# Last chunk of the second down projection: four token tiles in pairs, four one by one, the last one in column halves

## The chip, the cores and the metric

One core of a Trainium2 chip runs the whole program. The metric is the device time of one execution in microseconds. Engines are named as the profile names them: PE (TensorE matmuls), PEld (TensorE weight loads), DVE (VectorE), ACT (ScalarE), POOL (GpSimd) and SP (SyncE, whose queue issues nearly all DMAs).

## The reference, cut to what matters

The reference is one inference step of a two-layer decoder trunk on 1024 prompt tokens and 64 sample tokens, width 1024, in float32. Each layer ends in a convolutional feed-forward block:

```
def conv_ffn(x, buf, w_up, conv_w, conv_b, w_down):
    h = x @ w_up                                  # 1024 -> 2 x 2816
    ...                                           # 3-tap causal convolution over tokens -> hc
    gate, val = jnp.split(hc, 2, axis=-1)
    out = (jax.nn.gelu(gate) * val) @ w_down      # 2816 -> 1024
    return out, hp[:, -(CONV_W - 1):]
...
x = x + rmsnorm(f_out, p['f_post_g'][i])
```

The change touches the product with w_down of the second layer, its root-mean-square norm with the gain f_post_g, and the residual addition, which give the outputs y_prompt and y_sample and are the last work of the program.

## The kernel before, in words

**Numbers in two parts.** Every float32 operand of a large matmul is split into a high part (fp32r) and the rest (lo). ACT casts the high part (L150), DVE subtracts it (L151). A product is three matmuls: high by high, high by low, low by high (mm3, L815, L816, L817).

**The down projection** (class Down, function ffn_down). The 2816 rows of w_down are 22 blocks of 128, in six chunks: blocks 0 and 1, then five chunks of four. Tokens are eight tiles of 128 (numbers 0 to 7) and the tile NTT of 64 sample tokens. Each chunk adds its part of the sum to a float32 tile acc per token tile. A chunk of kind "p" is computed plainly, tile by tile (function plain): per tile 4 blocks x 3 matmuls x 2 column halves = 24 matmuls, and 2 additions of a PSUM tile to acc. A chunk of kind "s" uses a Strassen-type scheme on pairs of token tiles (function pair): blocks two by two, columns in halves, tokens in two tiles, and seven products in place of eight. A pair takes 7 products x 2 block pairs x 3 = 42 matmuls of 128x512, and 7 additions to acc (function add, L1437), with PSUM tiles that go on accumulating after an addition has read them. Before the change the second layer's last chunk is of kind "s", in the order LORD = (NTT, 0, 2, 4, 6), where 0 stands for the tiles 0 and 1, and so on. The first layer's last chunk is of kind "p".

**Staging.** The input of a step comes from a DRAM buffer gd through the SP queue. For a pair and each of two block pairs, stage loads a tile gr of 256 KB (L1363), POOL makes four sums and differences of it (L1368 to L1371), and ACT and DVE split seven 128x128 operands in three pieces of 256, 128 and 512 columns. For a plain step, stage loads 256 KB (L1350; L1354 for the sample tile) and splits 512 columns at once. The weights of a "s" chunk are b11, b21, b22 and four differences t1 to t4, per block pair, each 128x512; b12 itself is not kept.

**The tail of a token tile** (function tail_a, L847 to L861, from done). ACT squares acc and sums it (L830), DVE multiplies by the gain (L857), forms the mean (L121), ACT takes the root (L126), DVE the reciprocal and one refining step (L127, L136, L140), DVE scales and adds the residual (L860), and SP stores the tile (L861). A residual tile is fetched four tiles ahead (fetch, L1392). For tile 7 the gain, the scaling and the store go by halves of the columns.

**What sets the order.** The functions emit instructions in program order; a list scheduler then fixes the order on each engine: instructions that are ready and have their buffers come first by program order, so an instruction can be hoisted far ahead of its place in the program. Each engine and the SP queue then runs its list strictly in that order. Buffers: gr has 5 slots (loads, sums of POOL, the junk output of the squares), acc has 14 (accumulators, gain, some staged operands), xr and raw 2 each, PSUM 5 for products. In ffn_down, pairs emit the staging of the next step and the tails of earlier tiles after two of their seven products; after the last pair (tt == 6) the tails of the tiles 4 to 7 come behind all matmuls in program order.

Of the kernel before, what the change touches and what calls it, by code (L numbers as in the profile page):

```python
# [20 lines left out]
P = 128  # L21
# [52 lines left out]
def trunk_kernel(ctx, tc, I, O):  # L74
# [772 lines left out]
    def tail_a(y, tt, post, xsrc, xdst, last=False, rest=slice(0, D), aside=False, xr=None):  # L847


        t0, n = tokens(tt)  # L850
        if xr is None:
            xr = slot("xr")
            nc.sync.dma_start(xr[0:n], xsrc(tt))
        halves = (slice(512, D), slice(0, 512)) if last else (slice(0, D),)
        ss = square_sum(y[:, rest], n)
        for hs in halves if last else (rest,):
            V.tensor_tensor(y[:, hs], y[:, hs], post[0:n, hs], ALU.mult)  # L857
        r = rstd_from(pools["ph"], ss, 1, n, "n1", bufs=4, pre=sums.pop(tt, None), aside=aside, root=tail.root)
        for hs in halves:
            V.scalar_tensor_tensor(y[:, hs], y[:, hs], r[0:n], xr[0:n, hs], op0=ALU.mult, op1=ALU.add)  # L860
            nc.sync.dma_start(xdst(tt)[:, hs], y[:, hs])  # L861
# [213 lines left out]

    NPAR = 20
    NCV = 18
    LORD = (NTT, 0, 2, 4, 6)

    def conv_params(i):  # L1080

# [173 lines left out]
    class Down:  # L1255
# [6 lines left out]
        def __init__(self, i):  # L1262
            self.wv = I["w_down"][i].rearrange("(f p) d -> p f d", p=P)
            last = i == 0
            self.plan = [("p", 0, 2)] + [("s", f, 4) for f in (2, 6, 10, 14)] + [("p" if last else "s", 18, 4)]
            self.steps = []
            for c, (kind, f0, nf) in enumerate(self.plan):
                self.steps += [(c, tt) for tt in (ORDER if kind == "p" else LORD if c == len(self.plan) - 1 else (0, 2, 4, NTT, 6))]
            self.gx, self.ws, self.loads = {}, {}, {}
            fh, fl = [t.rearrange("p k t -> p (k t)") for t in (xh, xl)]  # L1270
            self.xq = [fh[:, 1024 * j : 1024 * j + 1024] for j in range(7)]
            self.xp = [fl[:, 1024 * j : 1024 * j + 1024] for j in range(3)]
            cut = lambda t, o, n: t[:, o : o + n]
            self.pc = [cut(fl, 3072 + 896 * j, 896) for j in range(6)] + [cut(fh, 7168, 896)]

            self.first = self.pc[1], self.pc[2], self.pc[0]
            self.np, self.staged = 2, 0

        def weights(self, c):
# [9 lines left out]
            for e in range(2):  # L1289
# [8 lines left out]
                for j, n in enumerate(self.WOP):  # L1298
# [10 lines left out]
                    ws[e, n] = hi, lo  # L1309
                    yield  # L1310

        def load(self, c, n=99):

            if c < len(self.plan):
                if c not in self.loads:
                    self.loads[c] = self.weights(c)
                for _ in range(n):
                    if next(self.loads[c], 0) == 0:
                        break
# [11 lines left out]
        def stage(self, k):  # L1331
            c, tt = self.steps[k]
            kind, f0, nf = self.plan[c]
            t0, n = tokens(tt)
            if kind == "p" or tt == NTT:

                w = n if tt < NTT else 10 * NB
                if k == 1:
# [42 lines left out]
    def ffn_down(dn, i, xsrc, xdst, norm):  # L1381
# [13 lines left out]
        def done(tt):  # L1395
# [8 lines left out]
            if norm:  # L1404
                tail.add(y, tt, post[0], xsrc, xdst)
            else:
                tail_a(y, tt, post[0], xsrc, xdst, tt == NTT - 1, xr=res.pop(tt))
                fetch(ORDER.index(tt) + 4)

        def plain(k, c, tt):  # L1410
            kind, f0, nf = dn.plan[c]
            n = tokens(tt)[1]
            if c == 0:
                acc[tt] = slot("acc")
            gx, ws = dn.gx.pop(k), dn.ws[c]
            pa = [psum(), psum()]
            for f in range(nf):
                wh, wl = ws[f]
                st, sp = f == 0, f == nf - 1
                if n == P:  # L1420
                    seq = ((gx[:, f, 0:P], wh), (gx[:, f, 0:P], wl), (gx[:, f, P : 2 * P], wh))
                else:
                    seq = ((gx[:, f, 0 : 2 * n], wh), (gx[:, f, 0 : 2 * n], wl))
                for j, (lt, wt) in enumerate(seq):
                    for h in range(2):
                        PE.matmul(pa[h], lt, wt[:, h * 512 : (h + 1) * 512],  # L1426
                                  start=st and j == 0, stop=sp and j == len(seq) - 1)
            for h in range(2):
                a = acc[tt][:, h * 512 : (h + 1) * 512]
                if c == 0:  # L1430
                    A.copy(a, pa[h])
                else:
                    V.tensor_tensor(a, pa[h], a, ALU.add)

        def add(tt, h, ps):
            a = acc[tt][:, h * 512 : (h + 1) * 512]
# [68 lines left out]
        for k, (c, tt) in enumerate(dn.steps):  # L1505
            kind, f0, nf = dn.plan[c]
            if c == nch - 1 and post[0] is None:
                post[0] = row_bcast(I["f_post_g"][i])
                for j in range(4):
                    fetch(j)  # L1510
            if kind == "p":
                dn.upto(k + 2)
                plain(k, c, tt)
                flush()
                if c == 0:
# [4 lines left out]
                dn.upto(k + 1)  # L1520
                finish()
            else:
                last = tt == 6
                g = pair(k, c, tt)
                for j in range(7):
                    if j == 2:
                        flush()
                        dn.upto(k + 1)
                        if not (norm is False and last):
                            finish()  # L1530
                    next(g)
                    if last and j != 2:
                        dn.load(c + 1, 1)
                if not last:
                    dn.load(c + 1, 1 if norm and c == nch - 2 else (3, 2, 2)[tt // 2])
                rest.append((g, c + 1 if last else nch))
            if c == nch - 1:
                ends += [tt] if kind == "p" or tt == NTT else [tt, tt + 1]
                if kind == "p":
                    finish()  # L1540
        flush()
        finish()
# [570 lines left out]
```

## Time and profile before

| | us |
|---|---|
| median of 3 runs | 2664.31 |
| lowest, highest | 2664.18, 2665.32 |
| profiled execution | 2665.99 |
| its span, first to last instruction | 2664.1 |

The granted clock over the span is 0.98 of full speed. The last chunk of the second down projection lies in about the last 60 us of the span; the profile has per-engine timelines there, a chain of waits followed back from the last instruction, and tables by stretch. A matmul's row shows when it starts and a modelled duration that overlaps the next one; the cost of one in a dense row of matmuls is the distance from start to start.

### The profile page before, as it was taken

What the parts mean: (1) busy time and instruction counts of PE and PEld (TensorE: products, weight loads), DVE (VectorE), ACT (ScalarE), POOL (GpSimd) and SP (SyncE); (2) the same over time, 40 slices, a digit from 0 to 9 for tenths busy, and PEclk for the clock granted to TensorE, in tenths of its full rate; (3) what the DMA queues carried; (4) which work ended last, traced back from release to release, by engine and by line L of the source; (5) the groups of instructions that cost most, each with busy time, mean ns of one, the idle gap of its engine ahead of it and who ended that gap; (6) DMA issues with size and microseconds to landing.
All of it is one profiled execution on the core that took longest, in us unless ns stands there. A gap on an engine that the chain in (4) does not pass through costs nothing.

```text
span 2664.1 us, 39516 instructions
## 1 busy us (share of the span) xinstructions
PE 2493.7 (94%) x14234; PEld 2199.5 (83%) x14234; DVE 1947.8 (73%) x3543; ACT 1281.0 (48%) x2597; POOL 661.2 (25%) x1062
## 2 busy tenths in 40 slices
PE   3778998999999999999999899999899999998997
PEld 2777876999999977788777788877799999996776
DVE  7994358677777789984222688875877777778999
ACT  6763234444444454354322677764544444444433
POOL 3220030111111176501201222113011111127571
PEclk9999998999999999999999899999899999999999
DMA  5443233122222233445646333325322222233334
GB/s 144 104 97 88 84 126 126 58 76 78 85 72 78 81 117 97 125 134 183 207 158 210 104 83 96 98 93 173 127 69 79 75 75 74 75 98 105 92 107 154
DMA packets 265688, 286.77 MB, mean 108 GB/s; under 512 B 42268, under 2 KB 212564, under 8 KB 265492
## 3 DMA queue, kind: packets, MB, share of 16 engines
q1 hardware_dynamic: 261892, 273.55, 33.3%
q0 software_dynamic: 3088, 9.77, 1.7%
q8 instruction: 113, 1.85, 0.3%
q10 hardware_dynamic: 512, 0.92, 0.1%
q14 instruction: 83, 0.68, 0.1%
HBM read 193.58 MB, written 70.93 MB: 99 GB/s over the span
## 4 chain that ended last, share of the span: by engine, by line
PE 58%; DVE 13%; DMA 4%; issue 4%; ACT 3%; POOL 3%; SPq 0%; DVEq 0%; ACTq 0%; POOLq 0%
PE mm L815 17%; PE mm L817 17%; PE mm L816 17%; DVE acc L1437 2%; PE mm L1426 2%; DVE xT_lo L151 2%; DMA gr<-gd 2%; DVE S L1907 1%; ACT S L1911 1%; DVE xT_hi L151 1%; DVE wst L151 1%; PE mm L1935 1%; PE tr L876 1%; DVE acc L860 1%; POOL xr L1306 1%
## 5 line engine op out<-in xcount | busy, mean ns | idle before, releaser
L815 PE MATMUL mm<-xT_hi,whi 128*128 128x384 f32 (+1 forms) x1408 | 457.0, 325 | 2.0 <-ACT acc L1154 1.7
L816 PE MATMUL mm<-xT_lo,whi 128*128 128x384 f32 (+1 forms) x1408 | 456.2, 324 | 1.4 <-DVE xT_lo L151 1.4
L817 PE MATMUL mm<-xT_hi,wlo 128*128 128x384 f32 (+1 forms) x1408 | 454.0, 324 | 0.0
L815 PEld LDWEIGHTS mm<-xT_hi,whi 128*128 128x128 f32 x1408 | 265.4, 189 | 3.8 <-ACT acc L1154 2.4
L816 PEld LDWEIGHTS mm<-xT_lo,whi 128*128 128x128 f32 x1408 | 265.7, 189 | 2.2 <-DVE xT_lo L151 2.1
L817 PEld LDWEIGHTS mm<-xT_hi,wlo 128*128 128x128 f32 x1408 | 265.3, 189 | 0.8
L1203 POOL COPY cvo<-acc 128x2 f32<-128x2 f32 x88 | 54.2, 616 | 814.1 <-ACT acc L1186 814.0
L815 PE MATMUL mm<-whi,xT_hi 128*128 128x512 f32 x608 | 242.9, 404 | 5.8 <-ACT whi L798 5.8
L1200 DVE SCALAR_TENSOR_TENSOR acc<-acc,cpar,acc 128x1104 f32<-128x1104 f32 x176 | 239.9, 1385 | 4.7 <-ACT acc L1198 4.7
L816 PE MATMUL mm<-wlo,xT_hi 128*128 128x512 f32 x608 | 242.8, 400 | 0.1
L817 PE MATMUL mm<-whi,xT_lo 128*128 128x512 f32 x608 | 242.2, 400 | 0.0
L150 ACT CAST whi<-raw 128x1024 fp32r<-128x1024 f32 x88 | 92.7, 1053 | 248.5 <-PE mm L817 245.1
L1437 DVE TENSOR_TENSOR acc<-mm,acc 128x512 f32<-128x512 f32 x279 | 184.3, 679 | 8.4 <-PE mm L817 8.1
L151 DVE TENSOR_TENSOR wlo<-raw,whi 128x1024 fp32r<-128x1024 f32 x88 | 107.7, 1224 | 103.5 <-PE mm L816 90.8
L815 PE MATMUL mm<-acc,whi 128*128 128x384 f32 x528 | 178.8, 339 | 2.5 <-DVE acc L1160 2.5
L817 PE MATMUL mm<-acc,wlo 128*128 128x384 f32 x528 | 178.9, 339 | 0.0
L816 PE MATMUL mm<-acc,whi 128*128 128x384 f32 x528 | 178.3, 338 | 0.0
L815 PEld LDWEIGHTS mm<-whi,xT_hi 128*128 128x128 f32 x608 | 115.3, 190 | 36.9 <-ACT whi L798 6.2
L816 PEld LDWEIGHTS mm<-wlo,xT_hi 128*128 128x128 f32 x608 | 115.2, 189 | 27.9 <-DVE wlo L799 0.8
L817 PEld LDWEIGHTS mm<-whi,xT_lo 128*128 128x128 f32 x608 | 114.9, 189 | 27.9 <-issue 0.8
L1198 ACT ACTIVATE acc<-acc,cpar 128x1104 f32<-128x1104 f32 x88 | 114.2, 1313 | 18.1 <-DVE acc L1169 11.9
L1186 ACT COPY acc<-mm 128x256 f32<-128x256 f32 x88 | 32.4, 369 | 183.7 <-PE mm L817 183.7
(575 smaller groups left out, 6311.6 us busy)
## 6 DMA issues: line engine op xcount, KB each, us to landing
raw<-in_w_up_dram SPq DMA_DIRECT2D x88, 512.0 KB
gd<-acc SPq DMA_DIRECT2D x44, 552.0 KB
raw<-in_w_down_dram SPq DMA_DIRECT2D x44, 512.0 KB
gr<-gd SPq DMA_DIRECT2D x80, 256.0 KB
raw<-in_glu_w_dram SPq DMA_DIRECT2D x40, 256.0 KB
acc<-in_cache_k_dram SPq DMA_DIRECT2D x16, 512.0 KB
acc<-in_cache_v_dram SPq DMA_DIRECT2D x16, 512.0 KB
xj<-in_x_prompt_dram SPq DMA_DIRECT2D x8, 512.0 KB
```

What stands on the lines that cost most here:

```text
L150: A.copy(hi_ap, ps_ap)
L151: V.tensor_tensor(lo_ap, ps_ap, hi_ap.bitcast(F32), ALU.subtract)
L815: PE.matmul(out, lh, rh, start=start, stop=False, **kw)
L816: PE.matmul(out, lh, rl, start=False, stop=False, **kw)
L817: PE.matmul(out, ll, rh, start=False, stop=stop, **kw)
L860: V.scalar_tensor_tensor(y[:, hs], y[:, hs], r[0:n], xr[0:n, hs], op0=ALU.mult, op1=ALU.add)
L1186: A.copy(hb[:, 2 + n0 : 2 + SEQ], ps[:, 0:wp])
L1198: A.activation(hc, hb[:, 2 : 2 + TG], AF.Identity, bias=cp[:, ft, 3:4], scale=cp[:, ft, 2:3])
L1200: V.scalar_tensor_tensor(hc, hb[:, tap : tap + TG], cp[:, ft, tap : tap + 1], hc, op0=ALU.mult, op1=ALU.add)
L1203: GP.tensor_copy(co[:, 0:2], hb[:, SEQ : SEQ + 2])
L1426: PE.matmul(pa[h], lt, wt[:, h * 512 : (h + 1) * 512], start=st and j == 0, stop=sp and j == len(seq) - 1)
L1437: V.tensor_tensor(a, ps, a, ALU.add)
```

## The change

The second layer's last chunk becomes a third kind, "m". Its order is NTT, 0, 2 (two pairs), then 4, 5, 6, 7 plainly, one by one. Since plain steps need b12 of each block pair, which the scheme does not keep, fourth loads it again (two DMAs of 256 KB into gr tiles) and splits it, during the first pair. Before each plain step the tails that are due are emitted, and only the next step is staged (one ahead; the first layer's plain chunk stages two ahead). Tile 7 is computed for its right column half first (12 matmuls), whose addition, squares and gain are done at once (part); then the left half, whose tail squares and multiplies only 512 columns. The gain of tile 7 was applied by halves already, so tail_a's loop over halves for it goes.

```
--- before.py
+++ after.py
@@ -853,8 +853,7 @@
             nc.sync.dma_start(xr[0:n], xsrc(tt))
         halves = (slice(512, D), slice(0, 512)) if last else (slice(0, D),)
         ss = square_sum(y[:, rest], n)
-        for hs in halves if last else (rest,):
-            V.tensor_tensor(y[:, hs], y[:, hs], post[0:n, hs], ALU.mult)
+        V.tensor_tensor(y[:, rest], y[:, rest], post[0:n, rest], ALU.mult)
         r = rstd_from(pools["ph"], ss, 1, n, "n1", bufs=4, pre=sums.pop(tt, None), aside=aside, root=tail.root)
         for hs in halves:
             V.scalar_tensor_tensor(y[:, hs], y[:, hs], r[0:n], xr[0:n, hs], op0=ALU.mult, op1=ALU.add)
@@ -1075,7 +1074,8 @@
 
     NPAR = 20
     NCV = 18
-    LORD = (NTT, 0, 2, 4, 6)
+
+    LORD = (NTT, 0, 2, 4, 5, 6, 7)
 
     def conv_params(i):
 
@@ -1262,10 +1262,10 @@
         def __init__(self, i):
             self.wv = I["w_down"][i].rearrange("(f p) d -> p f d", p=P)
             last = i == 0
-            self.plan = [("p", 0, 2)] + [("s", f, 4) for f in (2, 6, 10, 14)] + [("p" if last else "s", 18, 4)]
+            self.plan = [("p", 0, 2)] + [("s", f, 4) for f in (2, 6, 10, 14)] + [("p" if last else "m", 18, 4)]
             self.steps = []
             for c, (kind, f0, nf) in enumerate(self.plan):
-                self.steps += [(c, tt) for tt in (ORDER if kind == "p" else LORD if c == len(self.plan) - 1 else (0, 2, 4, NTT, 6))]
+                self.steps += [(c, tt) for tt in {"p": ORDER, "m": LORD, "s": (0, 2, 4, NTT, 6)}[kind]]
             self.gx, self.ws, self.loads = {}, {}, {}
             fh, fl = [t.rearrange("p k t -> p (k t)") for t in (xh, xl)]
             self.xq = [fh[:, 1024 * j : 1024 * j + 1024] for j in range(7)]
@@ -1309,6 +1309,26 @@
                     ws[e, n] = hi, lo
                     yield
 
+        def single(self, c, tt):
+            kind = self.plan[c][0]
+            return kind == "p" or kind == "m" and 4 <= tt < NTT
+
+        def fourth(self, c):
+
+            for e in range(2):
+                raw, u = slot("gr"), wslot("wst", F32R)
+                nc.sync.dma_start(raw, self.wv[:, self.plan[c][1] + 2 * e, 512:D])
+                hi, lo = u[:, 0:512], u[:, 512:1024]
+                split_evac(hi, lo, raw)
+                self.ws[c][e, "b12"] = hi, lo
+
+        def weight(self, c, f, h):
+
+            ws = self.ws[c]
+            if self.plan[c][0] == "p":
+                return [w[:, h * 512 : h * 512 + 512] for w in ws[f]]
+            return ws[f // 2, f"b{1 + f % 2}{1 + h}"]
+
         def load(self, c, n=99):
 
             if c < len(self.plan):
@@ -1332,7 +1352,7 @@
             c, tt = self.steps[k]
             kind, f0, nf = self.plan[c]
             t0, n = tokens(tt)
-            if kind == "p" or tt == NTT:
+            if self.single(c, tt) or tt == NTT:
 
                 w = n if tt < NTT else 10 * NB
                 if k == 1:
@@ -1404,7 +1424,8 @@
             if norm:
                 tail.add(y, tt, post[0], xsrc, xdst)
             else:
-                tail_a(y, tt, post[0], xsrc, xdst, tt == NTT - 1, xr=res.pop(tt))
+                last = tt == NTT - 1
+                tail_a(y, tt, post[0], xsrc, xdst, last, rest=slice(0, 512 if last else D), xr=res.pop(tt))
                 fetch(ORDER.index(tt) + 4)
 
         def plain(k, c, tt):
@@ -1412,25 +1433,28 @@
             n = tokens(tt)[1]
             if c == 0:
                 acc[tt] = slot("acc")
-            gx, ws = dn.gx.pop(k), dn.ws[c]
+            gx = dn.gx.pop(k)
             pa = [psum(), psum()]
-            for f in range(nf):
-                wh, wl = ws[f]
-                st, sp = f == 0, f == nf - 1
-                if n == P:
-                    seq = ((gx[:, f, 0:P], wh), (gx[:, f, 0:P], wl), (gx[:, f, P : 2 * P], wh))
-                else:
-                    seq = ((gx[:, f, 0 : 2 * n], wh), (gx[:, f, 0 : 2 * n], wl))
-                for j, (lt, wt) in enumerate(seq):
-                    for h in range(2):
-                        PE.matmul(pa[h], lt, wt[:, h * 512 : (h + 1) * 512],
-                                  start=st and j == 0, stop=sp and j == len(seq) - 1)
-            for h in range(2):
-                a = acc[tt][:, h * 512 : (h + 1) * 512]
-                if c == 0:
-                    A.copy(a, pa[h])
-                else:
-                    V.tensor_tensor(a, pa[h], a, ALU.add)
+
+            for hs in ((1,), (0,)) if kind == "m" and tt == NTT - 1 else ((0, 1),):
+                for f in range(nf):
+                    w = {h: dn.weight(c, f, h) for h in hs}
+                    st, sp = f == 0, f == nf - 1
+                    if n == P:
+                        seq = ((gx[:, f, 0:P], 0), (gx[:, f, 0:P], 1), (gx[:, f, P : 2 * P], 0))
+                    else:
+                        seq = ((gx[:, f, 0 : 2 * n], 0), (gx[:, f, 0 : 2 * n], 1))
+                    for j, (lt, o) in enumerate(seq):
+                        for h in hs:
+                            PE.matmul(pa[h], lt, w[h][o], start=st and j == 0, stop=sp and j == len(seq) - 1)
+                for h in hs:
+                    a = acc[tt][:, h * 512 : (h + 1) * 512]
+                    if c == 0:
+                        A.copy(a, pa[h])
+                    else:
+                        V.tensor_tensor(a, pa[h], a, ALU.add)
+                    if hs == (1,):
+                        part(a, tt, post[0], slice(512, D))
 
         def add(tt, h, ps):
             a = acc[tt][:, h * 512 : (h + 1) * 512]
@@ -1508,8 +1532,11 @@
                 post[0] = row_bcast(I["f_post_g"][i])
                 for j in range(4):
                     fetch(j)
-            if kind == "p":
-                dn.upto(k + 2)
+            if dn.single(c, tt):
+                if kind == "m":
+                    flush()
+                    finish()
+                dn.upto(k + (1 if kind == "m" else 2))
                 plain(k, c, tt)
                 flush()
                 if c == 0:
@@ -1520,23 +1547,25 @@
                 dn.upto(k + 1)
                 finish()
             else:
-                last = tt == 6
+                last = tt == (2 if kind == "m" else 6)
                 g = pair(k, c, tt)
                 for j in range(7):
                     if j == 2:
                         flush()
                         dn.upto(k + 1)
-                        if not (norm is False and last):
+                        if norm or kind == "m" or not last:
                             finish()
                     next(g)
                     if last and j != 2:
                         dn.load(c + 1, 1)
                 if not last:
                     dn.load(c + 1, 1 if norm and c == nch - 2 else (3, 2, 2)[tt // 2])
+                    if kind == "m":
+                        dn.fourth(c)
                 rest.append((g, c + 1 if last else nch))
             if c == nch - 1:
-                ends += [tt] if kind == "p" or tt == NTT else [tt, tt + 1]
-                if kind == "p":
+                ends += [tt] if dn.single(c, tt) or tt == NTT else [tt, tt + 1]
+                if dn.single(c, tt):
                     finish()
         flush()
         finish()
```

## Rows read from the trace of the kernel before

**Rows 1.** Stretches of the end: start:end, length, then busy time (and instructions) of PE, PEld, DVE, ACT and POOL, granted clock, DMA share, GB/s.
```profile
2600.00:2620.00 20.00, 20.00 (x88) 16.21 (x87) 20.00 (x38) 10.13 (x20) 6.95 (x10) 1.00 0.32 106
2620.00:2640.00 20.00, 20.00 (x87) 16.15 (x86) 18.98 (x36) 7.86 (x19) 4.63 (x10) 1.00 0.40 125
2640.00:2665.00 25.00, 9.25 (x33) 6.09 (x31) 20.78 (x46) 5.13 (x13) 0.00 (x0) 0.72 0.55 205
```

**Rows 2.** The chain that ended last, in order of time, its last part: start, duration, what.
```profile
2628.57 4.64 DMA gr<-gd
...
2650.23 1.22 DVE acc L857
...
2656.27 1.28 DVE acc L860
2657.55 1.20 DVE acc L857 x2
```

**Rows 3.** Timeline of PE, the last matmuls: start, duration, line, operation, operands; in brackets the idle time before and what ended it.
```profile
2640.02 0.39 PE L816 MATMUL mm<-xT_hi,xT_lo 128*128 128x512 f32 x1
2641.28 0.50 PE L817 MATMUL mm<-xT_hi,xT_lo 128*128 128x512 f32 x1 [0.87 <-DVE xT_lo L151]
...
2647.38 0.40 PE L817 MATMUL mm<-xT_hi,xT_lo 128*128 128x512 f32 x1
2650.37 0.50 PE L815 MATMUL mm<-wst,acc 128*128 128x512 f32 x1 [2.59 <-DVE acc L1437]
...
2651.81 0.63 PE L816 MATMUL mm<-xT_hi,xT_lo 128*128 128x512 f32 x1
2652.24 0.63 PE L817 MATMUL mm<-xT_hi,xT_lo 128*128 128x512 f32 x1
```

**Rows 4.** Timeline of DVE over the last stage (columns as in rows 3): its beginning, and its end behind the last matmul, with ACT's last squares.
```profile
2611.29 0.67 DVE L1403 TENSOR_TENSOR acc<-acc,gr 64x512 f32<-64x512 f32 x1
...
2654.01 0.68 DVE L1437 TENSOR_TENSOR acc<-mm,acc 128x512 f32<-128x512 f32 x1
2654.78 1.06 ACT L830 ACTIVATE gr<-acc 128x1024 bf16<-128x1024 f32 x1 [1.77 <-DVE acc L1437]
...
2657.47 1.29 DVE L857 TENSOR_TENSOR acc<-acc,acc 128x512 f32<-128x512 f32 x2
2658.67 0.15 DVE L121 TENSOR_SCALAR rv<-ss 128x1 f32<-128x1 f32 x1
2659.09 0.16 DVE L127 RECIPROCAL rr<-rs 128x1 f32<-128x1 f32 x1 [0.27 <-ACT rs L126]
...
2659.74 1.42 DVE L860 SCALAR_TENSOR_TENSOR acc<-acc,rr,raw 128x512 f32<-128x512 f32 x2
```

**Rows 5.** Timeline of DVE: additions in a row, the subtractions that stage one block pair of a pair with the instruction behind them, and the gain of a whole tile.
```profile
2588.24 1.87 DVE L1437 TENSOR_TENSOR acc<-mm,acc 128x512 f32<-128x512 f32 x3
...
2624.49 1.21 DVE L151 TENSOR_TENSOR acc<-gr,acc 128x256 fp32r<-128x256 f32 x3
2625.63 0.14 DVE L140 SCALAR_TENSOR_TENSOR rr<-rs,rr 128x1 f32<-128x1 f32 x1
...
2636.36 1.21 DVE L857 TENSOR_TENSOR acc<-acc,acc 128x1024 f32<-128x1024 f32 x1
```

**Rows 6.** Timeline of DVE while POOL makes the sums and differences of a staged pair, in order without a gap.
```profile
2619.51 0.38 DVE L140 SCALAR_TENSOR_TENSOR rr<-rs,rr 64x1 f32<-64x1 f32 x1
2619.82 0.68 DVE L1437 TENSOR_TENSOR acc<-mm,acc 128x512 f32<-128x512 f32 x1
2620.58 1.35 DVE L857 TENSOR_TENSOR acc<-acc,acc 128x1024 f32<-128x1024 f32 x1
2621.85 0.14 DVE L121 TENSOR_SCALAR rv<-ss 128x1 f32<-128x1 f32 x1
```

**Rows 7.** One group by line and shape, from 2611.24 on: line, engine, operation, tiles, count | busy us, mean ns | idle before.
```profile
L1371 POOL TENSOR_TENSOR gr<-gr,gr 128x128 f32<-128x128 f32 x4 | 2.9, 732 | 0.3
```

**Rows 8.** Timeline of PE in the first layer's last chunk, which is plain: two groups of a dense row, with two matmuls between them.
```profile
1164.55 1.07 PE L1426 MATMUL mm<-whi,acc 128*128 128x512 f32 x4
...
1165.91 1.07 PE L1426 MATMUL mm<-whi,acc 128*128 128x512 f32 x4
```

**Rows 9.** The same chunk: a load of one tile's input on SP, its cast on ACT and its subtraction on DVE.
```profile
1180.14 0.39 SPq L1350 DMA_DIRECT2D gr<-gd  x1
...
1184.30 0.62 ACT L150 CAST acc<-gr 128x512 fp32r<-128x512 f32 x1
...
1186.04 0.67 DVE L151 TENSOR_TENSOR acc<-gr,acc 128x512 fp32r<-128x512 f32 x1
```

**Rows 10.** Timeline of the SP queue in the last chunk: start, duration, line, DMA.
```profile
2614.97 0.43 SPq L1363 DMA_DIRECT2D gr<-gd  x1
2623.20 0.51 SPq L861 DMA_DIRECT2D out_y_sample_dram<-acc  x1
...
2624.39 0.59 SPq L1363 DMA_DIRECT2D gr<-gd  x1
```

**Rows 11.** PE at the beginning of the same down projection: a matmul after a wait (timeline), and two stretches behind it (columns as in rows 1).
```profile
2406.10 1.22 PE L1426 MATMUL mm<-whi,xT_lo 128*128 128x512 f32 x2 [3.45 <-ACT xT_lo L150]
...
2412.00:2414.00 2.00, 1.88 (x5) 1.50 (x5) 1.71 (x4) 0.62 (x1) 1.92 (x2) 0.50 0.91 313
2416.00:2418.00 2.00, 2.00 (x10) 1.60 (x9) 1.60 (x2) 1.68 (x6) 2.00 (x2) 1.00 0.02 8
```

## The prediction

> **What bounds the kernel now.** I read first the stretches of the end, then the chain of waits, then the timelines of PE and DVE there. In the stretches [rows 1] both PE and DVE are full from 2600 to 2620; from 2620 to 2640 PE is full and DVE has 1.02 us of gaps; behind 2640 DVE is busy for 20.78 of the 21.16 us up to its last instruction, PE for 9.25. So the end is DVE's. The chain [rows 2] says the same: behind a load of staged input at 2628.57 nearly every piece is a DVE instruction of the tails or an addition, to the gain of tile 7 at 2657.55. PE runs dry because of it [rows 3]: it waits 0.87 us for a subtraction of the staging and 2.59 us for an addition that stood in DVE's queue, and its last six matmuls then start 0.43 us apart, the pace of 1.2 GHz. Between the last matmul (2652.24 + 0.63) and the end of DVE's work (2659.74 + 1.42 = 2661.16) lie 8.3 us, in which the tails of tiles 4 to 7 crowd [rows 4]; from there the last store takes to 2664.1, 2.94 us.
>
> **The change part by part, on DVE from 2611.29 on** [rows 4], where the program has reached the first pair and the sample tile's tail.
>
> Additions: two pairs have 14, four plain tiles 8. Three in a row take 1.87 us with their overlap, 0.60 each [rows 5]: 6 x 0.60 = -3.6.
>
> Staging: the subtractions of one block pair take 2625.63 - 2624.49 = 1.14 us [rows 5], four of them 4.56; the four plain tiles need one of 512 columns each, 4 x 0.60 = 2.4. Together -2.2.
>
> b12: two subtractions of 512 columns, +1.2 on DVE; the casts lie on ACT, which is idle for more than half of each stretch [rows 1]. The two loads pass through SP and two gr tiles, before any plain step needs them; I cost that at nothing as long as the first pair's and second pair's matmuls (84, over 19 us at the pace below) cover them, and price its failure under the third rival.
>
> Halves: the gain of tile 7 was in halves before, so it costs nothing more; part adds one instruction of a column, +0.1, and ACT gets two squares of 512 for one of 1024.
>
> POOL: 16 sums and differences of two pairs go. While POOL works, DVE's small instruction took 0.38 instead of 0.14, the gain 1.35 instead of 1.21 and the addition between them 0.76 to the next start instead of 0.60 [rows 5, 6]. That is 0.5 us that I count, -0.5. The Trainium skill goes further (page "SBUF — State Buffer", section "SBUF: two separate sides"): VectorE and GpSimd share a port pair as an exclusive lock, and a VectorE instruction with two SBUF inputs waits for the whole GpSimd instruction. By that rule, taken at its worst with the mean of the longest POOL group, 0.73 us [rows 7], 16 x 0.73 = 11.7 us of DVE's time would come free, and PE's limit below would set the end. I take what the rows show: the slowed instructions are few, and none lost a whole POOL instruction.
>
> Idle time: DVE had 1.02 + 0.38 = 1.4 us of gaps [rows 1]. The first go, since no pair's staging is late any more; in their place stands the wait for ACT's squares behind the last addition (half of 1.06 plus its read-out, less the gain of 0.6 that runs beside it) and the small waits for the root as now. I take it as even; bounds -0.8 and +2.
>
> Tails of tiles NTT to 6, stores, residual fetches: the same instructions, earlier. Sum on DVE: -3.6 - 2.2 + 1.2 + 0.1 - 0.5 = -5.0 us.
>
> **On PE.** Two pairs have 84 matmuls, four plain tiles 96. Without its waits, PE would start its last matmul of before at 2640.02 + 31 x 0.2325 = 2647.2 (31 starts from 2641.28 to 2652.24 [rows 3]; 0.2325 is the pace of the dense stretch ahead, 20 us by 86 to 88 matmuls [rows 1]). Twelve more are +2.8; the plain ones go at (1165.91 - 1164.55) / 6 = 0.227 [rows 8], so 96 of them save 0.5. The last matmul starts at 2649.5 and ends near 2649.9. Then: addition 0.7, squares of half a tile some 0.75, and from the mean on as now 2664.1 - 2658.67 = 5.4 [rows 4]: 2656.8. PE alone would allow -7.3; with DVE's queue 2 us behind, DVE's -5.0 stands. A plain tile loads DVE with 2 additions, one subtraction, gain, scaling and 0.4 of small ones, 4.6 us in 24 x 0.227 = 5.4 us of PE, so the backlog of the pairs melts only by 0.8 us per tile.
>
> **Sum.** Span 2664.1 - 5.0 = 2659.1. The profiled execution took 2665.99, 1.9 more than its span and 1.7 more than the median, so it gives 2661.0 on its own scale; from the median, 2664.3 - 5.0 = **2659.3**. About 0.2% (5.3 us) is what a measurement of this kernel can tell from no change; the forecast lies just inside it.
>
> **Rivals.**
> *PE sets the end* (2656.5 to 2658.3, centre 2657.0). DVE is relieved by more than my sum, since its freed time falls where PE waited for it, and loses less to POOL; then 7.3 us are saved. For it: the last 31 matmuls lost 5 us to waits and the slow pace [rows 3], and plain tiles have no PSUM tile that must be read before it accumulates on. Against: DVE's gaps are only 1.4 us now [rows 1]. Chance 0.22. The rule of the Trainium skill's page "SBUF — State Buffer" on the shared port would lead here; the slowed instructions [rows 6] bear it out only in part.
>
> *Data a little late* (2660.5 to 2664.5). b12, or the input of one plain tile, arrives late once. From the issue of a plain tile's load to the end of its subtraction pass 1186.04 + 0.67 - 1180.14 = 6.6 us [rows 9], against 5.4 us of PE per tile. One tile staged one ahead and queued behind the store of the tile three before it would be 1 to 3 us late. For: loads did stand behind the store of the sample tile, from 2623.20 to 2624.39 [rows 10], and the chain passed through the next load [rows 2]. Against: a plain tile needs one gr slot instead of a pair's four. Chance 0.20.
>
> *SP's queue blocks* (slower, near 2675). SP issues strictly in order, and a store waits for its tile's scaling. A tile's store comes about one plain tile after its last matmul; if the loads of tiles 6 and 7 stand behind the stores of 4 and 5, each is 6.6 us late, 13.2 together. After such a wait PE restarts at half clock: behind a wait of 3.45 us, and a shorter one, the clock was still 0.50 six us later, and 1.00 ten us later [rows 11]; half of 48 matmuls at 0.43 instead of 0.227 are 4.9 more. PE ends at 2649.9 + 18.1 = 2668, the span 6.9 later, 2675: 10.6 slower. It decides where PE loses over 12.6 us: load 7 issued at 2638 or before costs nothing, at 2644.5 all of one tile. For: such an order in program text, one step ahead. Against: the scheduler hoists loads; the load at 2614.97 belongs to a pair whose place in the program comes two products into the pair before it [rows 10]. Chance 0.10, of it 0.02 within 0.2%.
>
> That the change does not do what it says: the right half's early work could sit behind earlier tails in DVE's queue, so that halving brings nothing. That is worth under 0.7 us and lies in the first case's range.
>
> **How the numbers follow.** The forecast (DVE's sum, 2658.0 to 2661.0) has 0.48, of it 0.20 below 2659.0; PE sets the end 0.22; a little late 0.20; SP blocks 0.10. Faster by over 0.2%: 0.20 + 0.22 = 0.42. Within: 0.28 + 0.20 + 0.02 = 0.50. Slower: 0.08. The range, 2656.5 to 2664.0, holds the first two cases and nearly all of the third, 0.86 by the bounds, which I shade to 0.8 for what the idle bound of +2 adds.
>
> **What would show it.** In the changed kernel's timeline: L1437 and its plain counterpart 6 fewer together; no POOL work behind the second pair; PE without waits from 2640 on at clock 1.00, its last matmul near 2650; DVE full to about 2656 with the last addition 1 to 3 us behind the last matmul. Wrong: gaps on PE before tiles 4 to 7 that end with a load or a subtraction (late data, SP blocks), or DVE with gaps before the last matmul (PE sets the end).

## The result, and the profile after

| | us |
|---|---|
| before, 15 runs beside the changed kernel | 2664.31 (2659.5 to 2668.01) |
| after, 15 runs | 2669.42 (2666.2 to 2673.38) |
| ratio after / before, 95% interval | 1.0023 [1.0016, 1.0030] |
| after: profiled execution; its span | 2669.42; 2667.7 |

Slower by 5 us, where 5 us faster was forecast. Positions in the span shift by some us between profiles: two profiles of one and the same order (e3 and f4 below) have the same step at 2606.69 and at 2610.61. So I count from a common origin, the start of the sample tile's first addition of its upper half to its lower one on DVE: 2611.29 in before [rows 4], 2610.02 in after.

The stretches of after, to be held against [rows 1] (same columns):

```profile
2600.00:2620.00 20.00, 20.00 (x88) 16.22 (x87) 20.00 (x37) 9.89 (x18) 0.62 (x1) 1.00 0.40 119
2620.00:2640.00 20.00, 12.52 (x54) 9.77 (x53) 18.54 (x39) 5.79 (x14) 0.00 (x0) 0.92 0.58 173
2640.00:2668.00 28.00, 18.31 (x72) 14.51 (x72) 16.01 (x31) 5.79 (x14) 0.00 (x0) 0.87 0.40 158
```

POOL is gone, as the edit meant, and up to 2620 both engines are as full as before. In the second stretch PE loses 7.5 us, where it had lost nothing. The timeline of PE says where; its end answers to [rows 3]:

```profile
2632.12 0.40 PE L817 MATMUL mm<-xT_hi,xT_lo 128*128 128x512 f32 x1
2640.36 5.39 PE L1449 MATMUL mm<-wst,acc 128*128 128x512 f32 x16 [7.84 <-ACT acc L150]
2645.58 0.40 PE L1449 MATMUL mm<-xT_hi,acc 128*128 128x512 f32 x1
...
2657.10 1.57 PE L1449 MATMUL mm<-xT_hi,acc 128*128 128x512 f32 x6
```

There is one wait of 7.84 us, ahead of tile 5's matmuls, for a cast of its input; tile 4 was done by then. The next 16 matmuls take 5.22 us from start to start (2640.36 to 2645.58; 3.72 at 0.2325 each), and from there PE runs densely to 2658.67. The wait of 2.59 us of before is gone. The input is late because of the SP queue (to be held against [rows 10]) and ACT:

```profile
2633.53 0.34 SPq L860 DMA_DIRECT2D out_y_prompt_dram<-acc  x1
2633.92 0.42 SPq L1412 DMA_DIRECT2D raw<-x3d  x1
2634.43 1.31 SPq L1370 DMA_DIRECT2D gr<-gd  x2
...
2643.80 0.39 SPq L1370 DMA_DIRECT2D gr<-gd  x1
```

```profile
2635.25 1.04 ACT L830 ACTIVATE gr<-acc 128x1024 bf16<-128x1024 f32 x1
...
2639.68 0.62 ACT L150 CAST acc<-gr 128x512 fp32r<-128x512 f32 x1 [1.56 <-DMA gr<-gd]
2640.80 0.62 ACT L150 CAST acc<-gr 128x512 fp32r<-128x512 f32 x1 [0.50 <-DMA gr<-gd]
```

The loads of tiles 5 and 6 are issued together at 2634.43, 1.9 us after PE ran dry at 2632.52, behind the store of tile 1, which waits for that tile's scaling on DVE. From the issue to PE's next matmul another 5.9 us pass, most of them for the transfer (5.17 in the chain below). The chain of after says the same, in order of time:

```profile
2628.80 2.34 PE mm L1449 x10
2634.43 5.17 DMA gr<-gd
2640.36 18.32 PE mm L1449 x72
```

DVE, whose queue the forecast took for the bound, then waits for PE; its end answers to [rows 4]:

```profile
2640.33 0.69 DVE L151 TENSOR_TENSOR acc<-gr,acc 128x512 fp32r<-128x512 f32 x1 [0.50 <-ACT acc L150]
...
2648.34 1.29 DVE L1455 TENSOR_TENSOR acc<-mm,acc 128x512 f32<-128x512 f32 x2 [5.00 <-PE mm L1449]
...
2658.70 0.69 DVE L1455 TENSOR_TENSOR acc<-mm,acc 128x512 f32<-128x512 f32 x1 [0.70 <-PE mm L1449]
...
2659.44 0.68 DVE L845 TENSOR_TENSOR acc<-acc,acc 128x512 f32<-128x512 f32 x1
2660.04 1.28 DVE L859 SCALAR_TENSOR_TENSOR acc<-acc,rr,xr 128x1024 f32<-128x1024 f32 x1
2661.24 0.68 DVE L856 TENSOR_TENSOR acc<-acc,acc 128x512 f32<-128x512 f32 x1
...
2662.90 1.41 DVE L859 SCALAR_TENSOR_TENSOR acc<-acc,rr,raw 128x512 f32<-128x512 f32 x2
```

DVE's last addition starts with PE's end, and in front of the last half's gain stand the first half's gain (L845) and tile 6's scaling (L859): the end is 9.0 us behind the last matmul.

The stretch from the origin to the end of DVE's last instruction, in before, in after, and in the kernel with free buffers (e3, below); columns as in rows 1:

```profile
2611.29:2661.16 49.87, 37.96 (x157) 29.32 (x155) 48.47 (x100) 19.30 (x43) 9.77 (x16) 0.90 0.46 160
```
```profile
2610.02:2664.31 54.29, 40.81 (x170) 32.38 (x168) 44.53 (x89) 18.36 (x39) 0.00 (x0) 0.93 0.47 158
```
```profile
2606.69:2654.64 47.95, 38.94 (x169) 31.29 (x167) 43.51 (x89) 17.96 (x39) 0.00 (x0) 0.94 0.49 154
```

DVE's work went from 48.47 to 44.53 and 43.51 us, -3.9 and -5.0. Its idle time went from 1.40 to 9.76 and 4.44 us. From the origin to the end of the span, last store included, it is 52.8 us in before, 57.7 in after and 52.8 in e3. That is the case in short: work left DVE, and idle time took its place.

### The profile page after: what moved, and what is told of

Its sections match the earlier page's. It is cut to its first block, busy times and chain, and to the rows that moved or that the text cites. A ratio compares the mean times of both kernels' runs of the same rounds, so it can differ in the third digit from the quotient of the medians.

```text
span 2667.7 us, 39512 instructions
## 1 busy us (share of the span) xinstructions
PE 2496.2 (94%) x14246; PEld 2203.5 (83%) x14246; DVE 1943.0 (73%) x3532; ACT 1278.6 (48%) x2593; POOL 648.9 (24%) x1046
## 4 chain that ended last, share of the span: by engine, by line
PE 63%; DVE 10%; DMA 3%; issue 3%; ACT 3%; POOL 2%; SPq 0%; DVEq 0%; ACTq 0%; POOLq 0%
PE mm L815 18%; PE mm L817 18%; PE mm L816 18%; PE mm L1449 3%; DVE S L1936 1%; DVE acc L1461 1%; ACT S L1940 1%; DVE xT_lo L151 1%; PE mm L1469 1%; DMA gr<-gd 1%; DVE wst L151 1%; DVE xT_hi L151 1%; PE mm L1964 1%; PE tr L875 1%; DVE S L1950 1%
## 5 line engine op out<-in xcount | busy, mean ns | idle before, releaser
L1461 DVE TENSOR_TENSOR acc<-mm,acc 128x512 f32<-128x512 f32 x265 | 175.0, 678 | 10.0 <-PE mm L817 9.7
```

What stands on the lines that cost most here:

```text
L1461: V.tensor_tensor(a, ps, a, ALU.add)
```

## The experiments

Theories: **S**, the SP queue issues strictly in order, and loads stand behind stores. **G**, a plain input needs a gr slot, which the squares' junk also uses; the program places its staging behind the tails of earlier tiles, so load and cast stand late in every list. **V**, with inputs in time DVE's tails set the end. Times are medians; the ratio is to the kernel before in the same runs.

**e1_two_ahead.** Plain inputs are staged two steps ahead, as in the first layer.

```
-                        dn.upto(k + 1)
+                        dn.upto(k + (2 if kind == "m" and last else 1))
...
-                dn.upto(k + (1 if kind == "m" else 2))
+                dn.upto(k + 2)
```

> The changed kernel, with plain tiles staged two ahead: the inputs of tiles 4 and 5 are emitted before the tails of tiles 0 and 1, those of 6 and 7 one step earlier each. In the SP queue the load of tile 5 then stands ahead of the stores of the sample tile and of tiles 0 and 1. Theory S (the loss is the load of tile 5 standing in SP's in-order queue behind the store of tile 1: 7.84 us of PE idle before tile 5 and about 1.6 us of matmuls at half clock): no PE wait over 1 us between tiles 4 and 7, clock 1.00 to the last matmul, about 9 us less than the changed kernel, 2659 to 2661, ratio to before 0.998. Theory V (the tails on DVE bound the end whatever PE does): PE's gap goes, but the end moves by less than 3 us, 2666 or more.

2665.8 us, 1.0001 [0.9990, 1.0012]. Neither S nor V came true: the wait did not go. The load of tile 5 (issued at 2612.80) went ahead of the sample tile's store, but the loads of 6 and 7 came only at 2634.72, behind the stores of tiles 1 and 2, and the wait moved to tile 6:

```profile
2634.72 1.80 SPq L1370 DMA_DIRECT2D gr<-gd  x2
```
```profile
2642.03 5.92 PE L1449 MATMUL mm<-wst,acc 128*128 128x512 f32 x16 [5.10 <-ACT acc L150]
```

**e2_pool_queue.** The plain loads go through GpSimd's queue; slots and program order stay.

```
-                    nc.sync.dma_start(gr, gd[...])
+                    (GP if kind == "m" else nc.sync).dma_start(gr, gd[...])
```

> The changed kernel, with the four loads of the plain tiles' inputs issued from GpSimd's queue, which has no other work there; program order and buffers as in the changed kernel. Theory S (SP's order): PE's gap before tile 5 goes, about 9 us less than the changed kernel, 2659 to 2661. Theory G (the load could not go earlier in any queue, because its gr slot is held until the junk output of a square is written): the gap stays above 5 us and the time is that of the changed kernel within 2 us, 2668 to 2671. Theory V: the gap goes and the time is 2666 or more.

2669.27 us, 1.0016 [1.0006, 1.0026], the time that G named: no store stands ahead of the loads, and PE still waits 6.16 us. The second load (tile 5) is issued at 2625.85, and its cast runs 20.7 us later, behind squares, in ACT's order; the third waits for a slot that squares hold:

```profile
2647.23 4.54 PE L1449 MATMUL mm<-wst,acc 128*128 128x512 f32 x12 [6.16 <-ACT acc L150]
```
```profile
2625.85 0.76 POOL L1370 DMA_DIRECT2D gr<-gd  x1 [4.17 <-DVE rr L127]
2636.13 0.75 POOL L1370 DMA_DIRECT2D gr<-gd  x1 [9.53 <-ACT gr L830]
```
```profile
2643.80 1.04 ACT L830 ACTIVATE gr<-acc 128x1024 bf16<-128x1024 f32 x1
...
2646.57 1.12 ACT L150 CAST acc<-gr 128x512 fp32r<-128x512 f32 x2
```

So S alone falls. There are two locks, one behind the other: the place of the load in SP's order, and the place of the cast in ACT's. With the first taken away the second holds PE nearly as long. In its plain form (the slot itself is held) G fits the third load, not tile 5's, which had its slot early.

**e3_free_buffers.** The plain inputs land in four pieces of a buffer that the chunk before used for weights, not in gr slots.

```
-                    self.gr0 = gr = slot("xr" if k in (2, 3) else "gr")
+                    if kind == "m" and tt < NTT:
+                        gr = self.xp[(tt - 4) // 2][:, 512 * (tt % 2) : ...].bitcast(F32)
+                    else:
+                        self.gr0 = gr = slot("xr" if k in (2, 3) else "gr")
```

> The changed kernel, with the plain tiles' loads going into a part of xT_lo that the chunk before has used up, in place of gr slots; same queue, same place in the program. They now stand ahead of all stores of this stage in SP's order. Theory G (gr slots decide where the scheduler puts the loads) and theory S (the place in SP's order decides the time) both expect PE's gap to go and 2658 to 2661, about 9 us less than the changed kernel; if e2 stays slow and this one is fast, G is the cause in execution; if both are fast, the slots only set the order. Theory V: 2666 or more.

2661.93 us, 0.9987 [0.9977, 0.9997]. All four loads are issued by 2603.01, ahead of every store (the first is at 2619.47), casts follow, and PE has no wait. G holds in the sense that the slot decides where the scheduler can put a load and its cast: nothing else was changed. PE's last matmul ends at 2645.62, 38.9 us behind the origin (before 41.6, after 48.7). But of the 9 us that G and S expected, 4.9 came (57.7 to 52.8 us from the origin to the end). DVE does not follow PE; its gaps stand ahead of the tails of tiles 3 to 6, and the last stores crowd:

```profile
2603.01 0.38 SPq L1373 DMA_DIRECT2D xT_lo<-gd  x1
```
```profile
2635.98 0.69 DVE L1464 TENSOR_TENSOR acc<-mm,acc 128x512 f32<-128x512 f32 x1 [1.71 <-PE mm L817]
2637.94 1.22 DVE L856 TENSOR_TENSOR acc<-acc,acc 128x1024 f32<-128x1024 f32 x1 [1.28 <-ACT gr L830]
...
2653.23 1.41 DVE L859 SCALAR_TENSOR_TENSOR acc<-acc,rr,raw 128x512 f32<-128x512 f32 x2 [0.30 <-DMA raw<-x3d]
```

PE's list has pair 2's last product among plain matmuls, at 2634.38, though the addition it waits for was done by 2628.8; so tile 3's last addition and tail come late.

```profile
2634.38 0.39 PE L815 MATMUL mm<-wst,xT_lo 128*128 128x512 f32 x1
```

The last store takes 2654.64 to 2659.5, 4.9 us, not 2.9; the DMA engines are full from 2649 to 2657 (busy share 0.95 to 1.07 in each 2 us), while in before the share is 0.36 from 2659 to 2661. One load still stands behind a store: tile 7's residual, issued at 2648.30 behind the store of tile 3, lands 4.84 us later, and the chain passes through it; it costs DVE the 0.30 us above.

**e4_no_halves.** After, with the last tile as a whole.

```
-            for hs in ((1,), (0,)) if kind == "m" and tt == NTT - 1 else ((0, 1),):
+            for hs in ((0, 1),):
...
-                tail_a(..., rest=slice(0, 512 if last else D), ...)
+                tail_a(..., rest=slice(0, D), ...)
```

> The changed kernel, with tile 7 not divided: 24 matmuls for both halves, one square of 1024 columns, one gain of 1024, stores in halves as before. It tells what the halving alone is worth. All theories keep PE's gap before tile 5. If halving works as meant, squares and gain of 512 columns less lie behind the last matmul: 0.6 on ACT, so 0.5 to 1.5 us slower than the changed kernel, 2670 to 2671. If the right half's early work stands in DVE's queue ahead of the last addition's followers (the changed kernel shows 2.4 us of such work between the last addition and the last mean), the time is the same within 0.5 or better.

2669.55 us, 1.0017 [1.0007, 1.0026], as after; PE's wait is 7.65 us. The halves bring nothing measurable here.

**f4_tails_later and f6_both**, and **f5_gain_pool, f7_e3_nohalves**, all on e3:

```
f4, f6:
-                        if norm or kind == "m" or not last:
+                        if norm or not last:
f5, f6 (pool: all tiles but 7):
-        V.tensor_tensor(y[:, rest], y[:, rest], post[0:n, rest], ALU.mult)
+        (GP if pool else V).tensor_tensor(y[:, rest], y[:, rest], post[0:n, rest], ALU.mult)
f7: the edit of e4
```

> The kernel with free buffers for the four plain inputs, and in it the tails of tiles 0 and 1 (squares, gain, scaling, store) written behind the last pair instead of behind the second, so that pair 2's staging and its additions come ahead of them in the queues of DVE and ACT. Theory V (with the inputs in time, DVE sets the end: some 14 us of tails are crowded behind the last matmul because tile 3's last addition comes at 2635.98, and DVE idles 0.83, 1.71 and 1.28 us ahead of them): the four idle stretches close and the tails of tiles 0 and 1 fill them, the work is the same, so the end comes up to 3 us earlier than with free buffers alone: 2659 to 2661 us. Rival B (DVE's sum of work behind the last pair is what bounds, and where the idle time lies makes no difference, or the tails of 0 and 1, some 5 us of DVE's work, just come later): 2662 to 2667 us.

> The kernel with free buffers, and in it the gain's multiply of the whole-width tails (tiles 0 to 6, 1.21 us each on DVE) on GpSimd, not DVE. Some four of these stand behind tile 3's last addition, so DVE has 4.8 us less to do there. Theory V (DVE sets the end): the last store is issued 3 to 5 us earlier, 2657 to 2659 us. Rival P (the end is set by each tile's latency, from its last addition through squares, gain and scaling to its store; GpSimd takes some 3 us for a multiply of 128x1024, by the rows of 128x512 in 1.56 us, instead of 1.21): no gain, 2661 to 2664 us. Rival D (the stores bound the end: five stores of 512 KB each are issued at 2649 to 2655 in the kernel with free buffers): under 2 us, 2660 to 2662 us.

> Free buffers, the tails of tiles 0 and 1 behind the last pair, and the gain's multiply on GpSimd. Theory V: both gains, 2655 to 2658 us, with the last matmul 43 us behind the third residual fetch and the end some 9 us behind that, not 14. Rival B: as the better of the two alone, or no better than free buffers alone (2662 us).

> Free buffers for the four plain inputs, and the last tile not by halves of its columns. With free buffers DVE is 14 us behind the last matmul, so its sum of work decides: the halves cost DVE a second set of small operations (0.14 us each) and a multiply in two parts, and give the first half's squares ahead of time. Theory V: no difference over 1 us, 2661 to 2663 us, since the tails of tiles 3 to 6 are ahead of the last tile's in any case. Rival H (the halving is what is worth something once the inputs are in time, as the prediction's part of 0.1 us did not count the latency of the last matmuls): slower by 2 us or more, 2664 us or later.

f4: 2665.12 us, 0.9998 [0.9987, 1.0009]; the scheduler gave every engine the same order as in e3, with the same gaps, so this is a second measurement of e3, and it too has 52.8 us from origin to end. The two ratios differ by 0.11%, as much as e3's gain: that e3 is faster than before is not shown. f6 is likewise f5 again: 2664.3 us, 1.0001 [0.9991, 1.0011], beside 2665.4 us, 1.0011 [1.0000, 1.0021]. So the question of where the idle time lies could not be tried this way. Taking the gain's multiply off DVE made nothing faster. Of the theories P comes nearest, but the rows show another reason than P's: GpSimd's multiplies stop DVE. POOL, then DVE:

```profile
2639.93 7.11 POOL L857 TENSOR_TENSOR acc<-acc,acc 128x1024 f32<-128x1024 f32 x3 [6.33 <-ACT gr L830]
```
```profile
2642.06 0.26 DVE L127 RECIPROCAL rr<-rs 128x1 f32<-128x1 f32 x2
2642.26 2.44 DVE L136 SCALAR_TENSOR_TENSOR rs<-rr,rv 128x1 f32<-128x1 f32 x1
2644.62 0.15 DVE L127 RECIPROCAL rr<-rs 128x1 f32<-128x1 f32 x1
2644.70 2.36 DVE L136 SCALAR_TENSOR_TENSOR rs<-rr,rv 128x1 f32<-128x1 f32 x1
```

An instruction of one column takes 2.44 us in place of 0.22, about a whole multiply of POOL (7.11 / 3 = 2.37). f7: 2661.8 us, 0.9994 [0.9984, 1.0003]: halves are worth nothing measurable in e3 either.

**g1_two_plain, g2_six_plain, g3_all_plain**: e3 with other numbers of plain tiles. The free buffers belong to kind "m"; in g3 the inputs are in gr slots again, staged two ahead.

```
g1:  LORD = (NTT, 0, 2, 4, 6, 7)             # single from tile 6 on
g2:  LORD = (NTT, 0, 2, 3, 4, 5, 6, 7)       # single from tile 2 on
g3:  the last chunk of kind "p" in both layers
```

> Three pairs and two plain tiles: the order is sample tile, 0, 2, 4 as pairs, then 6 and 7 one by one, with free buffers for the two plain inputs (the kernel with free buffers has 0, 2 and then four plain tiles). Against that kernel PE has 6 matmuls fewer (42 for 48, -1.4 us at 0.233 us each) and DVE three additions of 0.60 us more and about 1.1 us more of staging, the prediction's numbers for one pair. Theory V (once the inputs are in time DVE's work sets the end, PE is ahead by 7 us): 2 to 3 us slower than with free buffers and four plain tiles (two measurements of that gave 2661.9 and 2665.1), about 2664 to 2667 us. Rival T (what costs is that the tails of four plain tiles crowd behind the last matmul; with two they don't): faster than that by 1 to 3 us, 2660 to 2662 us.

> One pair and six plain tiles: sample tile, 0 as a pair, then 2 to 7 one by one, free buffers for all six plain inputs, the extra weights fetched in the first pair. Against four plain tiles with free buffers PE has 6 matmuls more (+1.4 us) and DVE three additions and about 1.1 us of staging less (-2.9 us); no last product of pair 2 is left that could come late and hold tile 3's tail. Theory V (DVE's work and its idle time behind the last matmul set the end): 3 to 5 us faster than with four plain tiles, 2657 to 2661 us. Rival T (tails crowd the more, the more tiles are plain, and the stores with them): no faster, 2663 to 2667 us. Where PE comes to set the end instead, its last matmul is 44 to 45 us behind the third residual fetch (43 with four plain tiles) and the end some 7 us behind that, 52 us, against 56.9 us: it would take over only below 2658 us.

> No pair in the last chunk at all: it is computed as the first layer's last chunk is (kind p, eight tiles and the sample tile one by one, inputs staged two ahead in the five gr slots that the squares' junk also uses, the last tile not by halves). PE has 12 matmuls more than with four plain tiles (+2.8 us), DVE six additions less and less staging (-5.8 us). Theory G (the inputs stand behind the squares that hold the gr slots): PE stalls for an input in the middle, some 3 to 8 us, and the time is 2664 to 2672 us, although DVE has the least work. Rival V alone (DVE's work decides and the inputs, two ahead, come in time as in the first layer): 2656 to 2661 us.

g1: 2662.75 us, 0.9999 [0.9987, 1.0011]. g2: 2663.79 us, 1.0001 [0.9990, 1.0012]. With two, four or six plain tiles and inputs in time the kernel is within about 0.1% of before: g1 lies between V and T, and V's 3 to 5 us for g2 did not come. In g2 PE waits 2.29 us for an addition, and its last matmul ends 44.5 us behind the origin. g3: 2657.74 us, 0.9980 [0.9971, 0.9989]; in this kernel the squares and the gain of tile 7's right half are left out. PE had no wait; G's stall did not come although the gr slots are shared.

**h1_all_plain_whole, h2_all_plain_halves**: g3 with that work in.

```
h1 (on g3): the edit of e4
h2 (on g3):
-            for hs in ((1,), (0,)) if kind == "m" and tt == NTT - 1 else ((0, 1),):
+            for hs in ((1,), (0,)) if not norm and c == nch - 1 and tt == NTT - 1 else ((0, 1),):
```

> The last chunk wholly plain, as the first layer's last chunk, with the last tile as a whole. (The run g3_all_plain left out the squares and the gain of the right column half of tile 7, some 0.6 us on DVE and 0.4 us on ACT at its end; here they are in.) There PE ran without a gap from 2570 to its last matmul, at 2648, and the end came 8.0 us behind it. Theory M (the stall of after comes from the mixed order, pairs and their staging ahead of plain tiles, and all plain tiles with inputs two ahead have none): PE as in that run, the end 1 to 2 us later than it, 2658 to 2660 us, below before by 0.15 to 0.25%. Rival O (the gain of that run was the work left out): 2662 to 2665 us.

> The same, and the last tile by halves of its columns, its right half's addition, squares and gain ahead of the left half's matmuls. In the all-plain kernel the tails come one per tile, DVE has idle time between them, and the end is 8 us behind the last matmul. If halving is worth something where the last tile's own tail is what is left (theory H), it takes the second addition's, half the squares' and half the gain's time from the end, 0.60 + 0.45 + 0.55 us: 1 to 2 us faster than the whole tile, 2656.5 to 2659 us. Rival Q (the halves' extra small operations and the gain of the first half stand in DVE's queue ahead of tile 6's scaling, as in after): within 1 us of the whole tile, or slower.

h1: 2660.82 us, 0.9988 [0.9978, 0.9997]. h2: **2659.83 us, 0.9977 [0.9967, 0.9986]**, of the kernels that do the whole work the one that is clearly faster than before, and than after. M holds for PE, though h1's gain is smaller than M said. In h2 PE is dense, DVE has gaps everywhere, and the end, 2659.8, is 8.9 us behind the last matmul (e3: 13.9):

```profile
2600.00:2620.00 20.00, 20.00 (x89) 16.39 (x88) 14.35 (x26) 6.38 (x11) 0.00 (x0) 1.00 0.21 62
2620.00:2640.00 20.00, 20.00 (x90) 16.57 (x89) 16.10 (x31) 6.99 (x15) 0.00 (x0) 1.00 0.72 232
2640.00:2662.00 22.00, 10.91 (x49) 8.69 (x47) 15.00 (x32) 4.89 (x12) 0.00 (x0) 0.80 0.30 116
```

PE nearly sets the end there: PE's last matmul ends at 2650.91, and the last addition starts 1.3 us later, behind tile 6's scaling and the first half's gain, which is near to what rival Q said:

```profile
2650.36 1.28 DVE L859 SCALAR_TENSOR_TENSOR acc<-acc,rr,xr 128x1024 f32<-128x1024 f32 x1
...
2651.62 0.68 DVE L845 TENSOR_TENSOR acc<-acc,acc 128x512 f32<-128x512 f32 x1
2652.22 0.68 DVE L1458 TENSOR_TENSOR acc<-mm,acc 128x512 f32<-128x512 f32 x1
```

Of the halves, there is 1.0 us between the medians; the intervals of h1 and h2 overlap, so their worth is likely, not shown.

Loads stand behind stores in h2 too. But the last input, tile 7's, is issued 8.0 us ahead of that tile's first matmul (near 2645.3), more than the 6.6 us that a load needs to the end of its subtraction:

```profile
2636.40 0.34 SPq L860 DMA_DIRECT2D out_y_prompt_dram<-acc  x1
...
2637.30 0.68 SPq L1373 DMA_DIRECT2D gr<-gd  x1
```

## Why the prediction was wrong

**DVE's sum held.** -5.0 was forecast; the work in the stretch fell by 5.0 in e3 and by 3.9 in after, with the same 89 instructions.

**PE's sum held, but for the stall.** The last matmul was forecast for 2649.9, that is 38.6 us behind the origin; e3 shows 38.9, after 48.7. Of the 9.7 us between these two, 7.84 are the wait and 5.22 - 16 x 0.2325 = 1.5 the slow pace; 0.4 stay open.

**The step that failed** is staging: its cost on DVE was counted (-2.2), and its place in the queues was put at nothing, with the lateness as rivals of 0.20 and 0.10. The runs show 7.84 us of wait in its place. The mechanism of these rivals was right: a load behind a store, 6.6 us from its issue to the end of the subtraction (2634.43 to 2641.02, the very time of [rows 9]). Both prices were wrong. "A little late" (1 to 3 us) took the load to wait for one store, in its turn; in fact the load of the second plain tile stood behind a store that waited for tile 1's tail, and was issued when PE had been dry for 1.9 us: 1.9 + 5.9 us. "SP's queue blocks" put the loads of tiles 6 and 7 behind the stores of 4 and 5; the load of 7 did stand behind the store of 4 (2643.80), and both came in time. The half clock, priced at 4.9 us behind two waits, cost 1.5 behind one. One wait of 7.84 in place of two of 6.6 gave 2669.4 (span 2667.7), between the rivals. The argument against, that the scheduler hoists loads, was the error: it hoists what has a free buffer. e2 shows that the load's queue alone did not decide, and e3 that the buffer, shared with the squares, decided for load and cast together. The row at 2614.97 [rows 10] showed a hoisted load, but not into which slot the next would go.

**Idle time as even** was the second miss. Even with inputs in time (e3) DVE idles 4.44 us where it had 1.40, +3.0, beyond the bound of +2; with the last store 1.9 us longer this takes back the 5.0: from origin to end it is 2664.1 - 2611.29 = 52.8 in before and 2659.5 - 2606.69 = 52.8 in e3. Cutting a queue's work moves the end only if the work behind is ready to move up. In e3's rows it hung on pair 2's late product; no run puts that product in place, and g2, which has no pair 2, was no faster (PE ended 44.5 us behind the origin there).

**PE sets the end** did not come with four plain tiles, but nearly does with all plain (h2). One reading was wrong without weight in the sum: of the last six matmuls of before (starts 2650.37, 2650.70, 2650.96 and on), the first two distances are 0.33 and 0.26 us, and only the others 0.42 to 0.43.

**POOL.** The term (-0.5) was not separated. Its reason, that no DVE instruction lost a whole POOL instruction, holds for before's short ones [rows 6], not in general: f5's rows show a whole one lost. In before the slowed L140 ends at 2619.89, as the POOL instruction beside it does (2619.88): it met that one part-way and lost 0.24 us, the rest of it.

```profile
2619.42 0.46 POOL L1370 TENSOR_TENSOR gr<-gr 128x128 f32<-128x128 f32 x1
```

The Trainium skill (page "SBUF — State Buffer", section "SBUF: two separate sides") states that of a GpSimd instruction and a DVE instruction with two SBUF inputs the one that starts first keeps the shared port pair for its whole length, and the other blocks. In f5 the trace agrees, 2.44 for 0.22 us.

**The halves** bring nothing measurable in after, as the last of the rivals said, and for its reason: L845 and tile 6's scaling stand ahead.

**b12** was in time: PE is full to 2620 in after, and tile 4's matmuls run before the wait.

Open: which trait of the all-plain order makes its loads early enough with the same gr slots (it stages two ahead, and its tails come one per tile; the two were not tried apart), and what an order with pair 2's product in place would give.

## What to carry to other kernels

For each transfer that an edit adds or moves, find the buffer it lands in, who held that buffer last, and what stands ahead of it and of its consumers in every in-order queue; price lateness from issue to use, against the moment at which the consumer runs dry. When work is taken off the bounding engine, ask what will be ready to fill the hole; otherwise it comes back as idle time. A mixed schedule has seams: here the uniform order, with more matmuls, was the faster one.

## What the hardware showed that was not expected

After 7.84 us without a matmul, PE took 0.33 us per matmul for the next 16, after 5.10 us (e1) 0.36, in place of 0.2325. In after the granted clock was 0.50 from 2640.36 to 2643 (1.2 GHz) and 1.00 from 2644 to 2657 (2.4 GHz); in e1 it was 0.50 from 2642 to 2646. So a stall's price was its length and 1.5 us (after) or 2.0 us (e1) more. And one-column DVE instructions lasted as long as the GpSimd multiply beside them (f5), while the reciprocals between them, with one input, took 0.15 us.
